# A hybrid attention and recurrence layer on one core: recurrence levels in pairs on two sets of key and query buffers, with moved loads, sigmoids and bias rows

## The chip, the core and the metric

The kernel runs on one core of one Trainium2 chip. A core has five engines with an instruction queue each: TensorE (PE, matmuls; PEld are its weight loads), VectorE (DVE), ScalarE (ACT), GpSimd (POOL) and SyncE (SP, which here only issues transfers), and 16 DMA engines move data between HBM and the on-chip memory (SBUF). Matmuls write to PSUM banks of 128 x 512 floats. The metric is the device time of one execution in microseconds (us); lower is better.

## The reference

One decoder layer on x of 1 x 1024 x 1024 in float32. The projection `h @ w_in` feeds two branches, which are gated and merged:

```python
mod = silu(c) @ w_ada + b_ada                      # shift, scale, gate
h = rmsnorm(x, norm_g) * (1 + scale) + shift
q_a, k_a, v_a, z_a, q_b, f_b, i_b, z_b, g_a, g_b = split(h @ w_in)
o_a = dilated_attention(q_a, k_a, v_a, rel_bias) * silu(z_a)       # 8 heads of 64
# recurrence, 8 heads, key and value width 128:
#   f = lb + (1 - lb) * sigmoid(f_b);  S_t = diag(f_t) S_(t-1) + (1 - f_t) i_t^T;  o_t = S_t^T silu(q_b)_t
o_b = rmsnorm(o_b, hgrn_onorm_g) * silu(z_b)
y = sigmoid(g_a) * (o_a @ w_branch_a) + sigmoid(g_b) * (o_b @ w_branch_b)
out = rmsnorm(x + gate * (y @ w_out), final_g)
```

The attention mixes three dilated windows; in the kernel this is one causal attention with a bias table (`toep`) that holds the relative bias and the logarithm of how many windows contain a distance.

## The kernel before

**Products.** All large products are done in two float parts, high and low: a step of a product is three 128x512 matmuls (`mm3`, lines 241, 242, 243: high by high, low by high, high by low). A weight piece of 128x512 is loaded (SP, L260), its high part is cast on ACT (`w_hi`, L248) and its low part subtracted on DVE (`w_lo`, L226). Products are done in pairs by a scheme with seven block products, whose sums run on DVE (L276) and copies on ACT (L329). They form a stream of steps. The attention and the recurrence are written as generators that yield an amount in microseconds; `fill(amount)` puts as many product steps of the stream between two pieces as `fill.rate` times the amount gives.

**Order.** PE's order is the order in which the program is written, throughout. In the start (lines 534 to 855) the orders of ACT, DVE and POOL are written by hand as well. Elsewhere a scheduler sets the orders of ACT, DVE, POOL and SP.

**Start (0 to some 76 us).** x arrives in eight tiles; each is squared and summed (`square_x`, L595/L597), the root taken with a power on POOL (`root_x`, L601), scaled (`scale_x`, L605 on ACT, L607 on DVE) and transposed (`turn_x` L624, `turn_late` L635). `mod_rows(c)` (L576) multiplies silu(c) with a quarter of w_ada that `load_wa(c)` loads, and copies the row (L579); `mod_turn(c)` (L586) turns it into columns, from which `make_h` (L650, L651, L654) makes the first operand `b11` (first half of the sequence) and `b12` (second half). `first_products` (L663, L664, L666) are the first three products, with weights that `split_first(n)` (L611) splits. `warm(n)` (L642) multiplies a tile of ones n times, to no use but keeping PE busy. `bias_row(b)` (L695) makes a third of the bias table on PE, `bias_add(b)` (L699) adds the logarithms on DVE.

**Attention (some 100 to 455 us).** Per head and query block: scores (L914, L915), bias and row maximum on DVE (L917), exp on ACT (L920), transposes, value products (L947). `load_head(h)` issues on POOL's queue the first half of a head's queries, keys and bias (`load_half`, L891, L897) and values (`load_value`, L902); the second half is loaded within `begin`. For head 0, the second half is held back by tiny casts on POOL (L889, L890) that read the first values tile `vq`. The values come from a turn (`ev_v`, L453 on ACT, L455 on SP) that writes a tile `vs` in SBUF and stores it to DRAM (`vq_d`).

**Branch a (some 455 to 555 us).** The attention output is gated and split (L1017 on DVE, L1019 on ACT) into operands `oah`, `oal`. Then `branch_a(m)`: `pre` loads g_a (L1029) and takes its sigmoid on ACT (L1030), when the unit's weights are prepared; `ev` multiplies the product with it, when the product ends.

**Recurrence (some 555 to 950 us, 8 heads).** The product of decays between two times is built by doubling: at level hl (1, 2, 4, ... 64) a block of 2 x hl times has keys in its first half and queries in its second. A level multiplies keys with queries (`small`, L1107, 32 matmuls of 32x32, or the wide form L1127 from 32 on), keeps the entries of that level (`copy_predicated`, L1120, or ACT copies into `amat`), multiplies the keys `kk` of the first halves (L1135) and the queries `qq` of the second halves (L1137; `qb` holds both queries and `qq`) with the decay of the other half, in place, and makes the decays of the next level (L1143, `tot`, `totn`). Each level ends with `yield 2.6`. Afterwards the keys are transposed (`kt`, L1159), the states made (`st`, L1171, L1175, L1177), the outputs (`pou`, L1186, L1188), their norm (L1191 to L1195; L1194 is a power on POOL) and, behind `yield 3.3`, their transposes (L1200) and the gate (L1202). The rest of the time, 950 to 1133, is branch b and the output product.

## Time and profile before

| what | value |
|---|---|
| time, median of 3 runs | 1131.35 us (1129.7 to 1131.97) |
| profiled execution | 1134.7 us |
| its span, first to last instruction | 1132.9 us |
| mean granted clock of TensorE | 0.994 |
| busy: PE, DVE, ACT, POOL | 1105.6, 807.6, 519.5, 123.1 us |

In the page's rows an engine's name stands ahead of its busy time, share of the span and number of instructions; small matmuls appear twice in the trace. The rows of a timeline have the start, the duration, the engine, the line and operation, out<-in with the shape and the count, and in brackets the idle time before and what ended it. Matmuls overlap, so the distance of two starts is the price of one, and not the duration. The rows of a stretch have the length, busy time and number of instructions, then the clock that TensorE was granted (1.00 is full), the share of the 16 DMA engines in use, and GB/s.

### The profile page before, as it was taken

What the parts mean: (1) busy time and instruction counts of PE and PEld (TensorE: products, weight loads), DVE (VectorE), ACT (ScalarE), POOL (GpSimd) and SP (SyncE); (2) the same over time, 40 slices, a digit from 0 to 9 for tenths busy, and PEclk for the clock granted to TensorE, in tenths of its full rate; (3) what the DMA queues carried; (4) which work ended last, traced back from release to release, by engine and by line L of the source; (5) the groups of instructions that cost most, each with busy time, mean ns of one, the idle gap of its engine ahead of it and who ended that gap; (6) DMA issues with size and microseconds to landing.
All of it is one profiled execution on the core that took longest, in us unless ns stands there. A gap on an engine that the chain in (4) does not pass through costs nothing.

```text
span 1132.9 us, 21754 instructions
## 1 busy us (share of the span) xinstructions
PE 1105.6 (98%) x8322; PEld 908.8 (80%) x8322; DVE 807.6 (71%) x1607; ACT 519.5 (46%) x1080; POOL 123.1 (11%) x207
## 2 busy tenths in 40 slices
PE   7999999999999999999999999999999999999997
PEld 6687788888888888788887878787887877888886
DVE  4487788878777776743788797978888773769053
ACT  5475555687555555632344444444453433334021
POOL 1103202303203201100000000000000012000000
PEclk9999999999999999999999999999999999999999
DMA  9739577646646624756725254443535389864052
GB/s 314 230 120 223 182 186 187 172 122 166 164 110 158 157 78 153 250 161 195 242 86 177 85 179 133 148 149 115 176 92 182 110 265 337 279 203 140 7 186 74
DMA packets 161608, 189.54 MB, mean 167 GB/s; under 512 B 11440, under 2 KB 107824, under 8 KB 161504
## 3 DMA queue, kind: packets, MB, share of 16 engines
q1 hardware_dynamic: 140080, 153.95, 42.5%
q0 software_dynamic: 21024, 33.60, 11.8%
q8 instruction: 65, 1.06, 0.4%
q10 hardware_dynamic: 400, 0.61, 0.2%
q14 instruction: 39, 0.32, 0.1%
HBM read 129.36 MB, written 58.76 MB: 166 GB/s over the span
## 4 chain that ended last, share of the span: by engine, by line
PE 88%; DVE 4%; DMA 3%; ACT 2%; issue 1%; POOL 1%; POOLq 0%; DVEq 0%; ACTq 0%; SPq 0%
PE m L241 18%; PE m L243 16%; PE m L242 16%; PE pq L243 5%; PE pq L242 5%; PE pq L241 5%; PE po L947 3%; PE pt L932 3%; PE pp L1107 3%; PE pss L915 1%; PE pss L914 1%; PE pou L1186 1%; DMA w_raw<-in_w_in_dram 1%; PE pou L1188 1%; PE pm L663 1%
## 5 line engine op out<-in xcount | busy, mean ns | idle before, releaser
L226 DVE TENSOR_TENSOR w_lo<-w_raw,w_hi 128x512 fp32r<-128x512 f32 x156 | 106.8, 687 | 55.5 <-ACT w_hi L248 52.5
L248 ACT CAST w_hi<-w_raw 128x512 fp32r<-128x512 f32 x146 | 90.5, 620 | 56.6 <-PE m L243 44.1
L329 ACT COPY ct<-m 128x512 f32<-128x512 f32 x90 | 52.7, 585 | 90.2 <-PE m L243 70.5
L248 ACT CAST w_hi<-w_s 128x512 fp32r<-128x512 f32 x90 | 55.9, 621 | 69.3 <-PE m L243 45.2
L276 DVE TENSOR_TENSOR ct<-m,ct 128x512 f32<-128x512 f32 x90 | 61.8, 687 | 24.6 <-PE m L243 24.2
L226 DVE TENSOR_TENSOR w_lo<-w_s,w_hi 128x512 fp32r<-128x512 f32 x90 | 61.9, 687 | 16.3 <-ACT w_hi L248 15.9
L920 ACT ACTIVATE s<-s,st 128x128 f32<-128x128 f32 (+3 forms) x64 | 49.8, 778 | 33.3 <-DVE st L917 33.3
L936 ACT CAST pth<-pt 128x512 fp32r<-128x512 f32 (+1 forms) x80 | 43.5, 544 | 36.6 <-PE pt L932 32.3
L226 DVE TENSOR_TENSOR ptl<-pt,pth 128x512 fp32r<-128x512 f32 (+1 forms) x80 | 50.6, 632 | 7.6 <-ACT pth L936 6.9
L1194 POOL TENSOR_TENSOR ssh<-ssh,halfh 128x4 f32<-128x4 f32 x16 | 18.0, 1128 | 340.4 <-DVE ssh L1193 340.4
L241 PE MATMUL m<-b11h,w_hi 128*128 128x512 f32 x124 | 52.4, 422 | 2.0 <-DVE ct L276 2.0
L241 PE MATMUL m<-b21h,w_hi 128*128 128x512 f32 x124 | 51.2, 413 | 0.0
L241 PE MATMUL m<-t2h,w_hi 128*128 128x512 f32 x120 | 49.9, 415 | 1.1 <-ACT ct L329 1.1
L241 PE MATMUL m<-b22h,w_hi 128*128 128x512 f32 x124 | 50.8, 410 | 0.0
L241 PE MATMUL m<-t1h,w_hi 128*128 128x512 f32 x120 | 50.2, 418 | 0.0
L241 PE MATMUL m<-t4h,w_hi 128*128 128x512 f32 x120 | 49.6, 413 | 0.4 <-DVE ct L276 0.4
L241 PE MATMUL m<-t3h,w_hi 128*128 128x512 f32 x120 | 49.6, 413 | 0.0
L243 PE MATMUL m<-b11l,w_hi 128*128 128x512 f32 x124 | 49.2, 397 | 0.0
L242 PE MATMUL m<-b11h,w_lo 128*128 128x512 f32 x124 | 49.2, 397 | 0.0
L243 PE MATMUL m<-b21l,w_hi 128*128 128x512 f32 x124 | 48.7, 393 | 0.0
L243 PE MATMUL m<-b22l,w_hi 128*128 128x512 f32 x124 | 48.7, 392 | 0.0
L242 PE MATMUL m<-b21h,w_lo 128*128 128x512 f32 x124 | 48.6, 392 | 0.0
(358 smaller groups left out, 3194.3 us busy)
## 6 DMA issues: line engine op xcount, KB each, us to landing
w_raw<-in_w_in_dram SPq DMA_DIRECT2D x128, 256.0 KB, 3.2
wa<-in_w_ada_dram SPq DMA_DIRECT2D x16, 512.0 KB, 8.9
qk_d<-ct SPq DMA_DIRECT2D x32, 256.0 KB, 4.2
k<-qk_d POOLq DMA_DIRECT2D x64, 128.0 KB, 4.7
toep<-toep_d POOLq DMA_DIRECT2D x16, 256.0 KB, 5.5
qp<-qk_d POOLq DMA_DIRECT2D x32, 128.0 KB, 4.9
vq_d<-ct SPq DMA_DIRECT2D x16, 256.0 KB, 3.5
vq<-vq_d POOLq DMA_DIRECT2D x16, 256.0 KB, 4.0
```

The costliest lines, as they stand in the source:

```text
L226: nc.vector.tensor_tensor(out_, a, hi.bitcast(F32), ALU.subtract)
L241: nc.tensor.matmul(ps, ah, bh, start=start, stop=False, skip_group_check=more)
L242: nc.tensor.matmul(ps, al, bh, start=False, stop=False, skip_group_check=more)
L243: nc.tensor.matmul(ps, ah, bl, start=False, stop=stop, skip_group_check=more)
L248: nc.scalar.copy(hi, src)
L276: nc.vector.tensor_tensor(out_, a, b_, op)
L329: nc.scalar.copy(c[name], b[which])
L920: nc.scalar.activation(s[:, :kw], s[:, :kw], AF.Exp, bias=prev, scale=-1.0, accum_out=st2[:, 2:3])
L932: nc.tensor.transpose(pt[:, c0:c0 + P], pn[b][:, kt * P:(kt + 1) * P], ident)
L936: nc.scalar.copy(pth[:, :w], pt[:, :w])
L947: nc.tensor.matmul(po[:, 256 - n:256], vq[kt // 4][:, kt % 4], src[:, c0:c0 + n], start=kt == 0 and a == 0, stop=kt == 2 * j + 1 and a == 1)
L1107: nc.tensor.matmul(pl[32 * b:32 * b + 32, c], kk[:, o:o + 32], qb[:, 2 - n:2, o:o + 32], start=True, stop=True)
```

## The change

- **Recurrence.** Level 1 runs alone, then levels (2, 4), (8, 16) and (32, 64) as pairs. A second pair of buffers for keys and queries (tiles named `kt` and `st`, whose memory later holds the transposed keys and the states; `st` has 8 slots now) takes what a level makes from the first: `grow` writes the multiplied halves into the other pair (DVE) and copies the unmultiplied halves (ACT). So within a pair both levels' operands exist at once and their matmuls are issued back to back. The second `grow` of a pair works in place. A head has eight new ACT copies of 128x512. The yield is 2.5 for each level, so 5.0 for a pair; the output's yield is 3.8, and the rate of filling is 34.0/34.6 of what it was.
- **First head's loads.** The second half's loads of head 0 are issued within `load_head(0)`, ahead of its value loads, and their casts read `vs`, the turn's tile in SBUF, in place of `vq`.
- **Sigmoid of branch a** is written in `ev`, ahead of the multiplication, in place of `pre`.
- **Start.** w_ada's first quarter is loaded ahead of the first weight piece; one bias row stays ahead of `mod_rows(0)`, one goes behind `mod_turn(0)`, one takes the place of ten of twelve warming matmuls. The first weight's cast and subtraction are taken apart and moved behind; the square of x7 and its root come ahead of the scalings; `mod_rows(1)` and `load_wa(3)` go ahead of the first products of the second half.
- **The turn of i** comes four product steps after its product in place of three.

The diff, cut: the old loop over the levels, which the section on the kernel before shows, and the bodies of `wide` and `keep`, which hold its matmuls from level 32 on and its copies unchanged, are left out, with two hunks of the start (the place of `load_wa(0)` and the bank of a bias row).

```diff
@@ -437,7 +437,7 @@
     def ev_k(p):
-    turned = {}
+    turned, last_v = {}, {}
     def ev_v(p, wait=2):
         def ev(src, th, psum):
@@ -453,6 +453,7 @@
                     nc.scalar.copy(vs[:, :, :, 0:E], got)
                     sub(vs[:, :, :, E:P], got, vs[:, :, :, 0:E])
                     nc.sync.dma_start(vq_d[p][:, 4 * th + n:4 * th + n + 2], vs.bitcast(F32))
+                    last_v[p] = vs
                 turned["v", p] = turned.get(("v", p), 0) + 1
             stream.after(wait, turn)
         return ev
@@ -469,7 +470,7 @@
-            stream.after(3, turn)
+            stream.after(4, turn)
@@ -606,12 +607,17 @@
+        def high_first(n):
+            firsts[n] = [wpool.tile([P, 4, P], F32R, name=name) for name in ("w_hi", "w_lo")]
+            nc.scalar.copy(firsts[n][0], stream.tiles[ids[n]])
+        def low_first(n):
+            sub(firsts[n][1], stream.tiles[ids[n]], firsts[n][0])
+            stream.done(ids[n])
-            hi, lo = (wpool.tile([P, 4, P], F32R, name=name) for name in ("w_hi", "w_lo"))
-            nc.scalar.copy(hi, stream.tiles[ids[n]])
-            sub(lo, stream.tiles[ids[n]], hi)
-            stream.done(ids[n])
-            firsts[n] = hi, lo
+            high_first(n)
+            low_first(n)
@@ -743,23 +748,22 @@
         scale_x(2, True)
         root_x(3)
         warm(8)
-        split_first(0)
         scale_x(3, False)
         turn_x(2)
         turn_x(3)
         keep_x(2)
         keep_x(3)
-        for b in range(2):
-            bias_row(b)
-        for b in range(2):
-            bias_add(b)
-        bias_row(2)
-        bias_add(2)
+        bias_row(0)
         mod_rows(0)
+        bias_add(0)
+        high_first(0)
         load_wa(2)
+        mod_turn(0)
+        bias_row(1)
+        low_first(0)
+        make_h(0, 0)
         stream.issue()
-        mod_turn(0)
-        make_h(0, 0)
+        bias_add(1)
         split_first(1)
         split_first(2)
         make_h(1, 0)
@@ -773,22 +777,24 @@
         root_x(4)
         root_x(6)
         root_x(5)
+        square_x(7, True)
+        root_x(7)
         scale_x(4, False)
-        square_x(7, True)
         scale_x(6, False)
-        root_x(7)
         scale_x(5, False)
         scale_x(7, True)
-        warm(12)
+        warm(2)
+        bias_row(2)
+        bias_add(2)
         turn_late(0)
-        main_banks(1)
-        first_products(0, (1,))
-        turn_late(1)
         mod_rows(1)
         load_wa(3)
-        first_products(1, (1,), (0,))
+        main_banks(1)
+        first_products(0, (1,), (0,))
+        turn_late(1)
+        first_products(0, (1,), (1, 2))
         mod_turn(1)
-        first_products(1, (1,), (1, 2))
+        first_products(1, (1,))
         make_h(2, 0)
         turn_late(2)
         first_products(2, (0,))
@@ -878,13 +884,16 @@
+            if h == 0:
+                load_half(h, 1)
         def load_half(h, c):
             if h == 0 and c == 1:
-                got = heads[h][4][0][:, 0, 0:1].bitcast(F32)
+                got = last_v[0][:, 0, 0, 0:1].bitcast(F32)
@@ -964,7 +973,8 @@
                     if i == 1:
-                        load_half(h, 1)
+                        if h > 0:
+                            load_half(h, 1)
@@ -1027,9 +1037,9 @@
-                    nc.scalar.activation(g[th], g[th], AF.Sigmoid)
             def ev(ps, th, psum):
+                nc.scalar.activation(g[th], g[th], AF.Sigmoid)
@@ -1099,55 +1109,77 @@
             dg = g1.tile([P, 256], F32, name="dg")
             d3 = c3(dg)
-            def small(n):
+            def small(n, k_, q_):
                 pl = pp.tile([P, 512], F32, name="pp")[:, :256 * n].rearrange("p (c n t) -> p c n t", c=8, n=n)
                 for c in range(8):
                     for b in range(4):
                         o = c * P + b * 32
-                        nc.tensor.matmul(pl[32 * b:32 * b + 32, c], kk[:, o:o + 32], qb[:, 2 - n:2, o:o + 32],
-                                         start=True, stop=True)
+                        to = pl[32 * b:32 * b + 32, c]
+                        if n == 2:
+                            nc.tensor.matmul(to, k_[:, o:o + 32], q_[:, :, o:o + 32], start=True, stop=True)
+                        else:
+                            nc.tensor.matmul(to[:, 0], k_[:, o:o + 32], q_[:, o:o + 32], start=True, stop=True)
                 return pl
...
+            def wide(hl, k_, q_):
...
+            def keep(hl, pl):
...
+            def halves(t, hl):
+                return t.rearrange("p (n two t) -> p n two t", two=2, t=hl)
+            def grow(fq, hl, a, b_):
+                n = S // (2 * hl)
                 t3 = fq[:, :2 * n].rearrange("p (n two) -> p n two", two=2)
+                for i in range(2):
+                    nc.vector.tensor_tensor(halves(b_[i], hl)[:, :, i], halves(a[i], hl)[:, :, i],
+                                            t3[:, :, 1 - i:2 - i].to_broadcast([P, n, hl]), ALU.mult)
+                    if a is not b_:
+                        nc.scalar.copy(halves(b_[i], hl)[:, :, 1 - i], halves(a[i], hl)[:, :, 1 - i])
+                tn = tots[hl.bit_length() % 2]
+                nc.vector.tensor_tensor(tn[:, :n], t3[:, :, 0], t3[:, :, 1], ALU.mult)
+                return tn
+            tots = tot, g1.tile([P, S // 2], F32, name="totn")
+            here, there = (kk, qq), (g1.tile([P, S], F32, name="kt"), g1.tile([P, S], F32, name="st"))
+            for levels in ((1,), (2, 4), (8, 16), (32, 64)):
+                got = []
+                if len(levels) == 2:
+                    fq = grow(fq, levels[0], here, there)
+                for hl, (k_, q_) in zip(levels, (here, there)):
+                    got.append(small(2, k_, qb) if hl == 1 else (small(1, k_, q_) if hl <= 16 else wide(hl, k_, q_)))
+                for hl, pl in zip(levels, got):
+                    keep(hl, pl)
+                if len(levels) == 2:
+                    fq = grow(fq, levels[1], there, there)
                 else:
+                    fq = grow(fq, 1, here, there)
+                here, there = there, here
+                yield 2.5 * len(levels)
+                if 4 in levels:
                     load_z(h)
+                if 16 in levels and h + 1 < NHB:
                     load_f(h + 1)
             for b in range(4):
                 nc.vector.tensor_copy(am[32 * b:32 * b + 32, :, 32 * b:32 * b + 32], d3[32 * b:32 * b + 32])
@@ -1161,7 +1193,7 @@
-            st_ = g1.tile([P, 7, P], F32, name="st")
+            st_ = g1.tile([P, 8, P], F32, name="st")
@@ -1193,7 +1225,7 @@
-            yield 3.3
+            yield 3.8
@@ -1210,7 +1242,7 @@
-        fill.rate = (len(stream.steps) - stream.at - 4) * 4 / NHB / 34.0
+        fill.rate = (len(stream.steps) - stream.at - 4) * 4 / NHB / 34.6
```

How the instructions stand on each engine, at three places. First PE in the start, from the last transposes of the first four x tiles (L624, now L630) to the first products (L663, now L669); L695 is a bias row and now L701, L576 is `mod_rows` and now L577, L586 is `mod_turn` and now L587. Before:

```order
L624 MATMUL pm_0_279<-kc,x_147 128x128 x4
L695 MATMUL pxt<-oh,rb 8x384
L695 MATMUL pmod<-oh,rb 8x384
L695 MATMUL pxt<-oh,rb 8x384
L576 MATMUL pmod<-wa_159,scz 32x256 x4
L576 MATMUL pmod<-wa_161,scz 32x256 x4
L576 MATMUL pmod<-wa_163,scz 32x256 x4
L576 MATMUL pmod<-wa_165,scz 32x256 x4
L586 MATMUL pmod<-kc,row 128x2 x2
L663 MATMUL pm_0_352<-b11h,w_hi 128x512
L664 MATMUL pm_0_352<-b11h,w_lo 128x512
L666 MATMUL pm_0_352<-b11l,w_hi 128x512
```

With the change:

```order
L630 MATMUL pm_0_275<-kc,x_147 128x128 x4
L701 MATMUL pxt<-oh,rb 8x384
L577 MATMUL pmod<-wa_157,scz 32x256 x4
L577 MATMUL pmod<-wa_159,scz 32x256 x4
L577 MATMUL pmod<-wa_161,scz 32x256 x4
L577 MATMUL pmod<-wa_163,scz 32x256 x4
L587 MATMUL pmod<-kc,row 128x2 x2
L701 MATMUL pxt<-oh,rb 8x384
L669 MATMUL pm_0_348<-b11h,w_hi 128x512
L670 MATMUL pm_0_348<-b11h,w_lo 128x512
L672 MATMUL pm_0_348<-b11l,w_hi 128x512
```

Two of the three bias rows have left the place ahead of `mod_rows(0)`; one of them stands behind `mod_turn(0)`. Further on, the second half of the start begins like this with the change (L648 is a warming matmul, L641 a late transpose):

```order
L672 MATMUL pm_0_350<-b11l,w_hi 128x512
L648 MATMUL pxt<-ones 128x128 x2
L701 MATMUL pxt<-oh,rb 8x384
L641 MATMUL pxt<-kc,t4h 128x128 x2
L641 MATMUL pxt<-kc,t4l 128x128 x2
L577 MATMUL pmod<-wa_177,scz 32x256 x4
L577 MATMUL pmod<-wa_179,scz 32x256 x4
L577 MATMUL pmod<-wa_181,scz 32x256 x4
L577 MATMUL pmod<-wa_183,scz 32x256 x4
```

Where twelve warming matmuls stood there are two and a bias row, and `mod_rows(1)` comes before any product of the second half.

Second, the recurrence. On PE, two levels of one head before, `pp` being the bank of a level's result, `kk` and `qb` its keys and queries:

```order
L1107 MATMUL pp<-qb,kk 32x32 x32
L241 MATMUL m_7214<-b21h,w_hi 128x512
L242 MATMUL m_7214<-b21h,w_lo 128x512
L243 MATMUL m_7214<-b21l,w_hi 128x512
L241 MATMUL m_7001<-t3h,w_hi 128x512
L242 MATMUL m_7001<-t3h,w_lo 128x512
L243 MATMUL m_7001<-t3l,w_hi 128x512
L241 MATMUL m_7001<-t3h,w_hi 128x512
L242 MATMUL m_7001<-t3h,w_lo 128x512
L243 MATMUL m_7001<-t3l,w_hi 128x512
L1107 MATMUL pp<-qb,kk 32x32 x32
L241 MATMUL m_7001<-t3h,w_hi 128x512
```

And a pair with the change (L1122; `kt` and `st` are the second pair of buffers):

```order
L243 MATMUL m_7261<-b21l,w_hi 128x512
L241 MATMUL m_7261<-b21h,w_hi 128x512
L242 MATMUL m_7261<-b21h,w_lo 128x512
L243 MATMUL m_7261<-b21l,w_hi 128x512
L1122 MATMUL pp<-qb,kk 32x32 x32
L1122 MATMUL pp<-st,kt 32x32 x32
L241 MATMUL m_7261<-b21h,w_hi 128x512
L242 MATMUL m_7261<-b21h,w_lo 128x512
L243 MATMUL m_7261<-b21l,w_hi 128x512
```

Nine product matmuls stood between two levels; now the two stand side by side. On DVE, between one pair's matmuls and the next pair's, in the same head (L1155 is the multiplication in `grow`, L1160 the next decays, L1139 the predicated copy; L226 and L276 belong to products):

```order
L276 TENSOR_TENSOR w_s<-w_s,w_raw_6213 128x512
L1139 COPY_PREDICATED dg<-kc,pp 128x256 x2
L1155 TENSOR_TENSOR kt<-kt,tot 128x32x16
L1155 TENSOR_TENSOR st<-st,tot 128x32x16
L226 TENSOR_TENSOR w_lo<-w_s,w_hi 128x512
L1155 TENSOR_TENSOR kk<-kt,totn 128x16x32
L276 TENSOR_TENSOR w_s<-w_raw_6147,w_s 128x512
L1155 TENSOR_TENSOR qb<-st,totn 128x16x32
L1160 TENSOR_TENSOR tot<-totn 128x16
```

Two predicated copies and four multiplications now follow each other, with product operations among them; before, one predicated copy and two multiplications stood between two levels.

Third, ACT in branch a, the casts of `oah` and the first sigmoids. Before (L1019 the cast, L1030 the sigmoid):

```order
L1019 CAST oah_4914<-oar 128x512
L329 COPY ct<-m_5032 128x512
L248 CAST w_hi<-w_raw_4948 128x512
L1030 ACTIVATE oar<-oar 128x512
L1019 CAST oah_4912<-oar 128x512
L1030 ACTIVATE oar<-oar 128x512
L1019 CAST oah_4914<-oar 128x512
L248 CAST w_hi<-w_s 128x512
L1030 ACTIVATE oar<-oar 128x512
```

With the change (L1029 the cast, L1042 the sigmoid):

```order
L1029 CAST oah_4904<-oar 128x512
L329 COPY ct<-m_5022 128x512
L248 CAST w_hi<-w_raw_4938 128x512
L1042 ACTIVATE oar<-oar 128x512
L1029 CAST oah_4902<-oar 128x512
L1042 ACTIVATE oar<-oar 128x512
L1029 CAST oah_4904<-oar 128x512
L248 CAST w_hi<-w_s 128x512
L1042 ACTIVATE oar<-oar 128x512
```

The scheduler's order is the same in both, though the sigmoid is written at another place.

60 lines of the change are left out of this document (20 added, 40 removed).

## The prediction

> **What bounds the kernel now.** I read the page first, then the waits of TensorE (PE), then stretches of the span with the granted clock beside the busy time. From the page, its engine row and its chain row:
>
> ```profile
> PE 1105.6 (98%) x8322; PEld 908.8 (80%) x8322; DVE 807.6 (71%) x1607; ACT 519.5 (46%) x1080; POOL 123.1 (11%) x207
> PE 88%; DVE 4%; DMA 3%; ACT 2%; issue 1%; POOL 1%; POOLq 0%; DVEq 0%; ACTq 0%; SPq 0%
> ```
>
> PE is the bound: 1105.6 of 1132.9 us, and 88% of the chain. So this edit can gain in three ways only: less idle time of PE (27.3 us, and it includes the first loads), fewer or closer matmuls, fewer stretches at a low clock. The waits, PE's line and tile, the releaser, then total us, times, longest:
>
> ```profile
> PE pss L914 <- DVE st L917: 2.5, 1, 2.5
> PE m L241 <- DVE ct L276: 2.5, 2, 2.0
> PE pt L1200 <- DVE kt L1195: 2.1, 2, 1.4
> PE pm L663 <- ACT b11h L650: 1.4, 1, 1.4
> PE m L241 <- ACT ct L329: 1.1, 1, 1.1
> PE pm L663 <- ACT b12h L650: 0.9, 1, 0.9
> PE pp L1127 <- DVE qb L1137: 0.6, 1, 0.6
> PE pm L663 <- ACT b11h L654: 0.5, 1, 0.5
> PE pp L1107 <- DVE qb L1137: 0.5, 1, 0.5
> ```
>
> One long wait each at the first attention score (L914) and in branch a (L241 for DVE's L276), three in the start (L663), and little in the recurrence (L1107, L1127, L1200). Waits cost more than their length. In these windows stand PE's time, its busy time and instructions, clock, DMA share, GB/s:
>
> ```profile
> 23.80:27.22 3.42, 1.75 (x6) 1.00 1.07 360
> 27.22:30.63 3.41, 3.41 (x10) 0.50 1.10 349
> 119.38:122.79 3.41, 0.91 (x4) 1.00 0.25 89
> 122.79:126.20 3.41, 3.27 (x13) 0.50 0.47 153
> 470.95:474.37 3.42, 1.37 (x7) 1.00 0.42 160
> 474.37:477.78 3.41, 3.41 (x8) 0.50 0.63 224
> ```
>
> Three times a window of 3.41 us in which PE is busy half or less is followed by 3.41 us at half clock. The last row holds 8 matmuls, 0.43 us each; the rows of the next fence start them 0.22 to 0.23 apart. Such a window therefore costs 8 x 0.20 = 1.6 us on top of the wait.
>
> **Part 1, the recurrence.** Rows of one level and of the product matmuls around it (start, duration), then the group's row:
>
> ```profile
> 616.33 0.39 PE L242 MATMUL m<-t3h,w_lo 128*128 128x512 f32 x1
> 616.55 0.39 PE L243 MATMUL m<-t3l,w_hi 128*128 128x512 f32 x1
> 616.87 0.76 PE L1107 MATMUL pp<-qb,kk 128*32 128x32 f32 x64
> 617.57 0.50 PE L241 MATMUL m<-b11h,w_hi 128*128 128x512 f32 x1
> 617.90 0.40 PE L242 MATMUL m<-b11h,w_lo 128*128 128x512 f32 x1
> L1107 PE MATMUL pp<-qb,kk 128*32 128x32 f32 x2048 | 24.4, 199 | 0.6 <-DVE qb L1137 0.5
> ```
>
> Going from 512-column matmuls to the small set and back costs time beyond the set. Entry: 616.55 to 616.87 is 0.32 instead of 0.23, +0.09. Leaving: the 64 records span 0.76 us and one takes 0.199, so they start (0.76 - 0.199)/63 = 0.009 apart; the next product could have followed 0.58 after 616.87, and came after 0.70, +0.13 (0.12 and the rounding). The first product after the set: 617.57 to 617.90 is 0.33 instead of 0.23, +0.10. Together 0.32 us for a switch. The change runs levels 2 and 4, 8 and 16, 32 and 64 back to back: 4 switches a head in place of 7, 24 fewer over 8 heads: **-7.7 us**. Bounds: -5 if the back-to-back sets have a seam of a third of a switch, -7.7 if none.
>
> What it adds on the other engines: eight copies of 128x512 on ACT for each head, 8 x 8 x 0.585 (the L329 row of the page, a copy of that size) = 37 us of ACT. Busy us of PE, PEld, DVE, ACT, POOL through six heads, and through the stretch in which DVE is fullest:
>
> ```profile
> 620.00:900.00 280.00, 277.42 (x3278) 225.65 (x3277) 229.98 (x446) 119.25 (x294) 13.50 (x12) 1.00 0.42 134
> 606.00:620.00 14.00, 13.48 (x240) 10.53 (x239) 13.51 (x26) 5.38 (x9) 0.00 (x0) 1.00 0.74 240
> L1120 DVE COPY_PREDICATED dg<-kc,pp 128x256 f32<-128x256 int32 x27 | 12.0, 443 | 2.1 <-PE pp L1107 2.0
> L1135 DVE TENSOR_TENSOR kk<-kk,tot 128x512 f32<-128x512 f32 x22 | 15.0, 683 | 0.1
> ```
>
> ACT goes from 119 of 280 to 119 + 6 x 8 x 0.585 = 147: it has room, so the copies are costed at nothing. If ACT were late, the second set of a pair would wait for a half that no product covers. DVE has less room, 82%, and its work per pair becomes one chain: 2 predicated copies and 4 multiplies, 2 x 0.44 + 4 x 0.60 (multiplies on DVE overlap: 0.68 long, 0.60 apart) = 3.3 us. In DVE's program order up to four product operations (0.6 each) stand inside that chain, so 3.3 to 5.7. The cover is 21 product matmuls at 0.228 = 4.8, and 0.6 of the sets themselves, 5.4. So a pair waits 0 to 0.3 on this account, 24 pairs: 0 to +7. Most pairs have at most two such operations inside (up to 4.5): I take **+1.5**.
>
> The last head's output transposes wait now:
>
> ```profile
> 945.50 0.63 PE L1200 MATMUL pt<-kc,kt 128*128 128x128 f32 x4 [1.36 <-DVE kt L1195]
> ```
>
> Nine product matmuls stand between its output products and these transposes; with the yield at 3.8 and a lower rate there are 15: 6 x 0.228 = 1.37, **-1.4** (0 if what follows DVE is late by as much). The other waits of L1107, L1127 and L1200 are 0.5 + 0.6 + 0.7 = 1.8; intervals of 5.0 in place of 2.6 cover about half: **-1** (0 to -1.8). Recurrence: -7.7 + 1.5 - 1.4 - 1 = **-8.6** (all better ends -10.9; all worse ends -5 + 7 = +2).
>
> **Part 2, the start.** Rows of PE, and one of ACT:
>
> ```profile
> 18.25 0.81 PE L695 MATMUL pxt<-oh,rb 32*8 32x384 f32 x2
> 20.44 1.94 PE L576 MATMUL pmod<-wa,scz 128*32 128x256 f32 x32
> 24.89 0.50 PE L663 MATMUL pm<-b11h,w_hi 128*128 128x512 f32 x1 [1.42 <-ACT b11h L650]
> 36.13 0.50 PE L663 MATMUL pm<-b12h,w_hi 128*128 128x512 f32 x1 [0.87 <-ACT b12h L650]
> 33.27 1.15 ACT L605 ACTIVATE t4l<-t4l,rs 128x1024 f32<-128x1024 f32 x1 [3.27 <-POOL rs L601]
> ```
>
> Three bias rows, from 18.25 up to mod_rows(0) at 20.44, (20.44 - 18.25)/3 = 0.73 each, stand on PE ahead of the modulation that the first product waits for; one is left: -1.5. The split of the first weight gives up its place on DVE ahead of the scaling of x3: -0.7 (one 128x512 subtraction, as long as the L1135 row's). So the first product comes at some 22.7 instead of 24.89, and the chain behind it moves with it: squares on ACT, powers on POOL, the last scaling on ACT (33.27 to 34.42) and the late transposes behind that. Ten of twelve warming matmuls go and a bias row comes in their place: nothing by itself, since the transposes wait for that scaling either way. mod_rows(1) then runs (1.9 us, as the first does) while ACT makes b12h, for which PE waited 0.87: -0.9. The wait for b11h of L654, 0.5, is covered likewise: -0.5. A bias addition that is now ahead of the second weight's split on DVE: +0.5. That makes -1.5 - 0.7 - 0.9 - 0.5 + 0.5 = -3.1. And the first half-clock window (27.22) may go, since its cause, the window with 1.75 us busy, holds that wait of 1.4 and may shrink with the work ahead of it: -1.6 as a whole, at an even chance -0.8. I take **-4** (-6 to -1: up to two of the small terms may fail, and the two warming matmuls leave PE without work for 1 to 2 us near 30, where another half-clock window would cost +1.6).
>
> The Trainium skill, page "TensorE: Matmul & The Clock Gate", section "HAM oscillation — how this bites in real kernels", puts the loss of clock behind idle gaps over about 3.4 us; by it, the thinner warm-up costs nothing. The windows above do not agree: no wait in the list is over 2.5 us, and three half-clock windows follow. By the page the start is -3.1 without regard to the clock, by the rows it is -4.7 or -1.5, as one window goes or one comes.
>
> **Part 3, the first head's loads.** DMA share in two stretches, three pieces of the chain of waits, and the first of the loads on POOL:
>
> ```profile
> 92.00:100.00 8.00, 6.87 (x35) 1.00 0.76 228
> 100.00:112.00 12.00, 12.00 (x58) 1.00 1.09 252
> 102.56 11.89 DMA w_raw<-in_w_in_dram
> 100.85 0.18 POOL L889 CAST qp<-vq 128x1 fp32r<-128x1 f32 x1 [0.83 <-DMA vq<-vq_d]
> 92.72 0.37 ACT L453 CAST ct<-pt 128x256 fp32r<-128x256 f32 x1 [0.55 <-DVE ct L226]
> ```
>
> From 100 on the DMA engines are full; a weight load issued at 102.56 takes 11.9 us, the chain that starts there ends at the score's 2.5 us wait, and a half-clock window follows: 2.5 + 1.6 = 4.1 to be had. The seven moved loads (one of 256 KB, six of 128 KB, 1 MB; at 252 GB/s some 4 us of traffic) go out behind L889's casts, which wait for vq until 100.85. Their gate becomes the v turn's tile in SBUF, which ACT writes at 92.72 to 93.09: they go some 7 us earlier, where the share is 0.76. On POOL's queue they pass the value load, which starts later by their issue. The weight then lands perhaps 4 us sooner, more than the wait. I take **-3** of -4.1 (to +1, if they lengthen the other wait here, the 1.1 for ACT's L329 near 96).
>
> The page "DMA: Bandwidth & Descriptors", section "Issuing engines are not separate DMA queues", of the Trainium skill says that all issuers share 16 engines and interleave. By that rule the megabyte merely takes its time elsewhere.
>
> **Part 4, the sigmoid at use.** Now ACT waits for a load ahead of casts that the products need:
>
> ```profile
> 471.73 0.63 ACT L1030 ACTIVATE oar<-oar 128x512 f32<-128x512 f32 x1 [5.79 <-DMA oar<-ga_d]
> 474.34 0.75 PE L241 MATMUL m<-b11h,w_hi 128*128 128x512 f32 x1 [2.05 <-DVE ct L276]
> ```
>
> 2.05 + 1.6 = 3.7 us would go. But ACT's order is set by the scheduler, and it puts each sigmoid at the very place among the casts where it was. **-0.7**, the gain only if the load lands earlier by chance (bounds -3.7 and 0). The i turn one product later moves four transposes by 0.7 us beside products: 0.
>
> **Sum.** -8.6 - 4 - 3 - 0.7 = -16.3. The profiled execution took 1134.7 (span 1132.9), so 1118.4 (span 1116.6); the median of the runs, 1131.35, lies 3.35 below it, and becomes **1115**.
>
> **The rivals.** (a) *The pair's second set waits* (slower). If ACT's copies or DVE's chain end late at each of the 24 pairs, 16.3/24 = 0.68 us of wait undoes everything; at the 0.9 by which a chain of 5.7 passes 4.8 of cover alone, it is -16.3 - 1.5 + 21.6 = +3.8: 1135. For it: DVE is busy 13.51 of 14 us in one stretch. Against it: 82% over six heads, and few operations inside most chains. (b) *Start and loads give nothing*: a half-clock window takes the place of the start's waits, and the loads fill the DMA engines 7 us earlier instead of later. Then only -8.6 - 0.7 are left: 1122; with the loads alone in vain, 1118. For it: the DMA share is 0.76 already where they go. (c) *Branch a's wait goes too*, by an earlier landing, and the start keeps its clock: -16.3 - 3 - 2 = -21.3: 1110. Against it: ACT's order. (d) *The switches do not get cheaper*, the seam between two sets being as dear: -16.3 + 7.7: 1123; with (b), 1130. For it: no row shows two different sets back to back. Against it: in the rows a switch costs beside a 512-column matmul. That part 4 does not do what it says is in the forecast.
>
> **How the numbers follow.** Forecast 0.52; (c) 0.18; (b) or (d) 0.19; both, no change, 0.04; (a) 0.07. The time is the forecast's, 1115. The range goes down past (c) with the recurrence's better end, 1106, and up past (b) and (d), 1125. A measurement here tells about 0.2% (2.3 us) from no change: faster 0.89, same 0.04, slower 0.07.
>
> **What would show it.** Right: 32 sets of small matmuls instead of 56, product matmuls before and after them as above and no wait of L1122 or L1131 over 0.5; mod_rows(1) ahead of the first late product; the first score's wait under 1 us and full clock after it; the 2-us wait of branch a still there. Wrong: PE waits for kt, st, kk or qb at most pairs; half-clock windows at new places near 30; ACT's or DVE's share in the recurrence at 95%.

## The result and the profile after

The changed kernel takes 1123.45 us (median of 4 runs, 1121.71 to 1124.08) against 1131.3 (4 runs, 1129.7 to 1131.97): a ratio of 0.9937, 95% interval 0.9924 to 0.995. In a second comparison it took 1121.94 (6 runs) against 1129.84 (29 runs), ratio 0.9932, 0.9917 to 0.9947. So it is faster by 0.6 to 0.7%: 7.1 to 7.7 us by the ratios, 7.9 by the medians, where 16.3 us were forecast. The direction and the range (1106 to 1125) held; the size is less than half. Two executions far outside the rest, 1461 us of the kernel before and 3850 us of an experiment below, are left out of all comparisons.

The profiled execution took 1122.96 us, with a span of 1121.1: 11.8 less than the span before. The engine row of its page, and seven of the waits of PE (line and tile, releaser, that is what ended the wait, then total us, times, longest):

```profile
PE 1095.0 (98%) x8302; PEld 905.4 (81%) x8302; DVE 806.8 (72%) x1607; ACT 555.2 (50%) x1144; POOL 124.6 (11%) x207
```

```profile
PE m L241 <- issue: 1.9, 1, 1.9
PE m L241 <- DVE ct L276: 1.9, 4, 0.9
PE pt L1232 <- ACT ct L470: 1.8, 1, 1.8
PE m L242 <- issue: 1.5, 1, 1.5
PE m L241 <- ACT w_hi L248: 1.2, 1, 1.2
PE pp L1122 <- DVE qb L1155: 1.0, 1, 1.0
PE pp L1122 <- issue: 0.4, 1, 0.4
```

The wait of 2.5 us for the first scores is gone, and a new one, for a weight's cast (L248), stands some 20 us ahead of its place. The 2.0 us wait of branch a is gone too. New is a releaser that the list of before does not have for PE: "issue", time in which PE waited for nothing that the profile shows, 1.9 + 1.5 + 0.4 us.

To see where time went, I cut each trace at the starts of the same PE instructions: the first product of the stream (L241), the last value product of the attention, the first small matmul of the recurrence, the first product of branch b (`pq`). Stretches in us, of the two profiles of before (the second belongs to an experiment below) and two of the change, counted from PE's first instruction, 1.0 us after the span's start:

```
                    start   products+attention   branch a   recurrence   end
before              76.26   364.75               116.45     390.40       176.62
before, again       78.89   364.53               113.55     390.27       177.08
change              71.89   362.60               113.87     386.43       177.90
change, again       71.42   363.21               114.52     386.35       176.99
```

The start lost 4.4 us against the profile on which the forecast was made, the attention 2.1, branch a 2.6, the recurrence 4.0, and the end gained 1.3. Forecast were 4, 3, 0.7, 8.6 and 0.

### The profile page after: what moved, and what is told of

It reads as the page before. It is cut to its first block, busy times and chain, and to the rows that moved or that the text cites. A ratio compares the mean times of both kernels' runs of the same rounds, so it can differ in the third digit from the quotient of the medians.

```text
span 1121.1 us, 21828 instructions
## 1 busy us (share of the span) xinstructions
PE 1095.0 (98%) x8302; PEld 905.4 (81%) x8302; DVE 806.8 (72%) x1607; ACT 555.2 (50%) x1144; POOL 124.6 (11%) x207
## 4 chain that ended last, share of the span: by engine, by line
PE 78%; DVE 8%; issue 7%; DMA 3%; ACT 2%; POOL 1%; POOLq 0%; DVEq 0%; ACTq 0%
PE m L241 15%; PE m L243 15%; PE m L242 15%; PE pq L241 4%; PE pq L242 4%; PE pq L243 4%; PE po L956 2%; PE pt L941 2%; PE pp L1122 2%; PE pss L924 1%; PE pss L923 1%; DVE w_lo L226 1%; PE pou L1218 1%; PE pm L669 1%; PE pm L672 1%
## 5 line engine op out<-in xcount | busy, mean ns | idle before, releaser
L226 DVE TENSOR_TENSOR w_lo<-w_raw,w_hi 128x512 fp32r<-128x512 f32 x156 | 106.7, 686 | 61.2 <-ACT w_hi L248 60.7
L248 ACT CAST w_hi<-w_raw 128x512 fp32r<-128x512 f32 x146 | 90.5, 621 | 43.0 <-PE m L243 29.7
L248 ACT CAST w_hi<-w_s 128x512 fp32r<-128x512 f32 x90 | 55.9, 621 | 56.4 <-PE m L243 37.5
L329 ACT COPY ct<-m 128x512 f32<-128x512 f32 x90 | 52.6, 585 | 57.3 <-PE m L243 52.8
L276 DVE TENSOR_TENSOR ct<-m,ct 128x512 f32<-128x512 f32 x90 | 61.7, 686 | 24.4 <-PE m L243 24.1
L226 DVE TENSOR_TENSOR w_lo<-w_s,w_hi 128x512 fp32r<-128x512 f32 x90 | 61.7, 686 | 12.3 <-ACT w_hi L248 11.4
L226 DVE TENSOR_TENSOR ptl<-pt,pth 128x512 fp32r<-128x512 f32 (+1 forms) x80 | 50.5, 631 | 7.4 <-ACT pth L945 6.6
L241 PE MATMUL m<-t4h,w_hi 128*128 128x512 f32 x120 | 49.5, 412 | 3.3 <-issue 1.9
L241 PE MATMUL m<-b11h,w_hi 128*128 128x512 f32 x124 | 50.8, 410 | 0.2 <-DVE ct L276 0.2
L241 PE MATMUL m<-b22h,w_hi 128*128 128x512 f32 x124 | 50.9, 410 | 0.0
L241 PE MATMUL m<-t3h,w_hi 128*128 128x512 f32 x120 | 49.5, 412 | 1.2 <-ACT w_hi L248 1.2
L241 PE MATMUL m<-b21h,w_hi 128*128 128x512 f32 x124 | 50.5, 408 | 0.0
L242 PE MATMUL m<-b22h,w_lo 128*128 128x512 f32 x124 | 48.5, 391 | 1.5 <-issue 1.5
L241 PE MATMUL m<-t2h,w_hi 128*128 128x512 f32 x120 | 49.2, 410 | 0.6 <-ACT ct L329 0.6
L241 PE MATMUL m<-t1h,w_hi 128*128 128x512 f32 x120 | 49.4, 412 | 0.3 <-DVE ct L276 0.3
```

The costliest lines, as they stand in the source:

```text
L226: nc.vector.tensor_tensor(out_, a, hi.bitcast(F32), ALU.subtract)
L241: nc.tensor.matmul(ps, ah, bh, start=start, stop=False, skip_group_check=more)
L242: nc.tensor.matmul(ps, al, bh, start=False, stop=False, skip_group_check=more)
L248: nc.scalar.copy(hi, src)
L276: nc.vector.tensor_tensor(out_, a, b_, op)
L329: nc.scalar.copy(c[name], b[which])
```

## The experiments

**The two kernels once more.** First the kernel before, unchanged.

> The kernel before, unchanged, profiled once more. Theory A (the profiled execution of before was longer than its other runs because branch a's load came late in it): the wait of L241 for DVE's L276 in branch a is under 1 us here, the first score's wait of 2.5 us is there again, and the span is about 1129.5. Rival B (both waits belong to the kernel): the wait of 2 us and the half-clock window behind it are there again, and the span is about 1133.

Span and clock of its profiled execution, and two of PE's waits in it:

```profile
core 0: 1132.7 us, clock 0.991
```

```profile
PE pss L914 <- DVE st L917: 2.5, 1, 2.5
PE m L241 <- DVE ct L276: 0.8, 2, 0.4
```

Theory A's first half holds: the first scores wait again, branch a does not. Its second half, a span of 1129.5, does not hold: the start took 2.6 us more, with 13.7 us at half clock (19.3 to 33.0) where the first profile had 3.4. The timed runs say why one profile is a poor base here. The 37 runs of the kernel before in this comparison (29 of the reference, 8 of this copy), by the granted clock that each lists:

```
clock            runs   median us   range
0.991 to 0.994     6    1134.3      1132.9 to 1137.2
0.995              8    1131.1      1129.1 to 1132.9
0.996              8    1129.65     1127.6 to 1133.9
0.997, 0.998      15    1129.15     1127.3 to 1131.4
```

The profile that the forecast used had 0.994: it belongs to the slowest sixth.

The Trainium skill, page "TensorE: Matmul & The Clock Gate", section "Part 1: The HAM clock gate", says that the window in which activity is watched is free-running and does not begin with the kernel. The traces agree: in the first profile the half-clock stretches begin 3.3 us past a multiple of 3.413 us from the first instruction (27.2, 122.8, 474.4), in the second 2.2 us past one (19.3, 125.1). Which idle time is followed by such a stretch is not settled by that. The kernel with the recurrence's part alone (below) has two windows of this kind, each with a wait of 1.9 us and nearly the same busy time, and full clock behind the first (it has 1.00 from 120.65 on), half clock behind the second:

```profile
117.24:120.65 3.41, 1.58 (x7) 1.00 0.56 202
642.90:646.31 3.41, 1.54 (x10) 1.00 0.51 187
646.31:649.72 3.41, 3.41 (x11) 0.50 0.68 246
```

Then the change, unchanged.

> The change, unchanged, once more. Theory A (PE runs out of instructions: its three stalls with no releaser all stand at instruction 256 k + 448, where a fetched block of 256 begins): stalls without a releaser, 2 to 5 us in all, in the recurrence again and at instructions of that form, though their length may differ, since the fetch shares the DMA engines; time 1123.5. Rival B (a disturbance of that one execution): no such stall, or at other counts, and a span about 4 us shorter, 1117.

It took 1121.94 us, with 3.3 us of waits without a releaser: theory A.

**What PE waits for when it waits for nothing.** In the change, two pairs of level sets and what follows them (start, duration, idle time before with its releaser):

```profile
751.51 0.76 PE L1122 MATMUL pp<-qb,kk 128*32 128x32 f32 x64
752.12 0.75 PE L1122 MATMUL pp<-st,kt 128*32 128x32 f32 x64
754.78 0.39 PE L241 MATMUL m<-t4h,w_hi 128*128 128x512 f32 x1 [1.90 <-issue]
...
842.55 0.76 PE L1122 MATMUL pp<-st,kt 128*32 128x32 f32 x64
843.21 0.75 PE L1122 MATMUL pp<-qb,kk 128*32 128x32 f32 x64
843.90 0.50 PE L241 MATMUL m<-b22h,w_hi 128*128 128x512 f32 x1
845.90 0.39 PE L242 MATMUL m<-b22h,w_lo 128*128 128x512 f32 x1 [1.50 <-issue]
```

Both stand behind a pair. Of the DMA queues just ahead of the first of these gaps and in its beginning, 751.6 to 753.5 us (packets, MB, share of 16 engines):

```profile
q8 instruction: 1, 0.02, 5.2%
```

That one packet is PE's instructions: 65 packets of 16,384 bytes on this queue in the whole execution, for 16,783 recorded instructions of PE and its weight loads, 256 to a packet. Counting those instructions from the start and numbering the packets k = 0, 1, ..., I find each packet's start, its end, and where the longest gap between two PE instructions near it falls:

```
profile            k    packet us         PE's gap stands at count    gap us
change             27   599.55-600.54     256 x 27 + 448              0.6
change             42   751.77-753.36     256 x 42 + 448              2.0
change             50   843.57-844.55     256 x 50 + 448              1.9
change, again      27   601.01-601.98     256 x 27 + 448              1.1
change, again      37   704.30-705.25     256 x 37 + 448              0.7
change, again      42   754.04-755.17     256 x 42 + 448              1.4
change, again      50   843.40-845.12     256 x 50 + 448              1.0
```

Each gap stands at the very instruction 256 k + 448, and ends 1.1 to 1.4 us after packet k has landed. In quiet stretches a packet starts when PE is some 155 instructions past 256 k, so PE has 293 more before it runs dry. A pair takes 256 of them within 1.3 us (128 records of matmuls and as many of weight loads). No record shows when a packet is asked for. If it is at that instruction 155, and PE can go on 1.4 us after the landing, then from asking to use takes 3.3 to 6.9 us in this stretch (an estimate from the packets' times; tenth to ninetieth percentile of 32 packets). Level 1's 128 instructions and the first pair's 256 are only 9 to 12 product matmuls apart. Of the Trainium skill, the page "Runtime: NRT & Kernel Launch", section "Instruction fetch mechanics", says that instructions come in blocks of 16 KiB, 256 of them, which the packets confirm; it also says that this fetch is hidden, since issue is slower than the filling, and the rows above show the opposite for dense small matmuls.

**Shifting the count.** If this is right, only the count of instructions ahead matters.

```diff
         warm(20)
+        ps = px.tile([P, 512], F32, name="pxt")
+        for n in range(58):
+            b = n % 4 * 32
+            nc.tensor.matmul(ps[b:b + 32, 0:32], ones[:, 0:32], ones[:, 0:32], start=True, stop=True)
```

> The change with 58 tiny matmuls (32x32, of ones) at a place in the first 12 us where PE waits for x: they cost no time, but every later instruction of PE comes 232 places later, so that the boundaries of fetched blocks fall on others. Theory A (PE stalls where a block of 256 instructions begins while the fetch is late, at 256 k + 448 by count): the stalls at 601, 752 and 844 us are gone, any new ones stand at 256 k + 448 of the new count; worked out from the trace, boundaries with less than 5.5 us between trigger and need are 3 in place of 7, so 1 to 3 us less than the change: 1119 to 1121. Rival B (a pair of sets stalls by itself, whatever the count): the same three places, 1122.

The gaps at 42 and 50 are gone, and the only ones left without a releaser, 0.8 us in two, stand at other places (the larger at 256 x 33 + 448, the smaller at 256 x 37 + 448). From the waits in the recurrence, 560 to 935 us:

```profile
PE pt L1236 <- ACT ct L470: 1.8, 1, 1.8
PE pp L1126 <- DVE qb L1159: 1.0, 1, 1.0
PE pp L1126 <- issue: 0.8, 2, 0.6
```

The recurrence took 383.55 us in place of 386.4, 2.9 less. The time is 1120.51 (ratio 0.9903, 0.9882 to 0.9925), 1.4 less than the change in the comparison before: my tiny matmuls were not free. They stood ahead of transposes whose x was already there, and the first product of the stream came at 74.50 in place of 71.4 to 71.9. So I put them behind `warm(4)`, where PE waits 1.4 us for x1 in every profile above.

> The change with the 58 tiny matmuls behind the four warming ones, where PE waits 1.4 us for x1 in every run, in place of behind the first twenty, where they delayed the start by 2.1 us. Theory A (the count alone takes the stalls for instructions away, worth 2.9 us in the recurrence): start as in the change, 71 to 72.5, recurrence 383 to 384, time 1118.5 to 1120. Rival B (what the recurrence gains comes back elsewhere): 1121 or more.

1120.01 us (0.991, 0.989 to 0.993); recurrence 382.73, start 72.39, no wait without a releaser of over 0.3 us. The recurrence's 3.7 us are confirmed; of the time 1.9 us arrive. In the profile the rest went to a wait of 1.9 us of the first `pq` products for DVE (`gbr`) with a half-clock stretch of 3.41 us behind it; whether the ordinary run has that too is not shown.

**Spreading the levels.**

```diff
-                yield 2.5 * len(levels)
+                yield 4.0 if 64 in levels else 4.5
```

> The change with yields of 4.5, 4.5, 4.5 and 4.0 behind the four groups of levels, in place of 2.5, 5, 5 and 5: more product matmuls between level 1 and the first pair, fewer between pairs. Theory A (256 + 128 instructions of level 1 and the first pair within 4 us are what drains PE's store of instructions): stalls without a releaser under 1 us in all, 1 to 3 us less than the change, 1119 to 1121. Rival C (the chain on DVE fills the interval between pairs): waits of the small matmuls for kt, st, kk or qb rise to 3 us or more, 1123 or more.

No wait without a releaser is left, and the first waits of the recurrence are

```profile
PE pt L1232 <- ACT ct L470: 1.8, 1, 1.8
PE pt L1232 <- DVE kt L1227: 0.9, 2, 0.8
PE pp L1131 <- DVE tot L1160: 0.6, 1, 0.6
```

The recurrence took 382.42 us. Waits of small matmuls for DVE are 0.8 us in all: rival C, DVE's chain, is out. The time is 1120.47 (0.9905, 0.9884 to 0.9927), with 2 to 3 us given back behind the recurrence (end 179.92).

**The recurrence alone, and all but the recurrence.** The first is the kernel before with the hunks of the diff from `dg = g1.tile` on; the second is the change without them.

> The kernel before with the recurrence's part of the change alone. Theory A (the switches saved 7.6 us as forecast, 1.6 come back at seams between the two sets of a pair and 3 to 5 as stalls for instructions): 3 to 5 us less than before, 1126 to 1128, with stalls without a releaser behind pairs. Rival B (the forecast's sum for the recurrence holds, and the rest of the change gave less than its profile shows): 8.6 less, 1122.7. Rival C (DVE's chain outlasts the cover): waits of L1122 for kt, st, kk or qb of 5 us or more in all.

> The change with the recurrence as before: start, first loads, sigmoid and the turn of i alone. Theory A (start -4.4 and attention -2.1 as the two profiles show, branch a the same in an ordinary execution): 5 to 7 less than before, 1124.5 to 1126.5. Rival B (forecast's recurrence): only about 0 to 2 less, 1129.5 to 1131, so that the whole is 1123.5 with -8.6 in the recurrence.

The recurrence alone gives 1128.29 (ratio 0.9985, 0.9972 to 0.9998), the rest alone 1127.82 (0.9981, 0.997 to 0.9992). Neither theory had this: -1.7 and -2.1 by the ratios do not add up to -7.7. The traces explain a part. The rest alone leaves out 40 PE instructions in the start (ten warming matmuls), and in it the old recurrence stalls for instructions too, within a set:

```profile
755.84 0.73 PE L1117 MATMUL pp<-qb,kk 128*32 128x32 f32 x60
757.62 0.26 PE L1117 MATMUL pp<-qb,kk 128*32 128x32 f32 x4 [1.05 <-issue]
```

This is at 256 x 41 + 448; its recurrence took 391.35 us, 1.0 more than before. The recurrence alone took 388.19, with a half-clock stretch at 646 us behind a wait of 1.9 us for ACT's L469 (the change has that wait, 1.8 us, without the stretch), and with 2.0 us of stalls in four places, the longest, 1.0, at 256 x 27 + 448. I tried to take the stall out of the rest alone.

> The change with the recurrence as before and ten tiny matmuls in the first 12 us, which give every later instruction of PE the place that it has in the kernel before, modulo 256. Theory A (the change's 40 instructions less in the start had brought a stall for instructions into the old recurrence too, and so the parts alone gave less than the whole): the stall near 755 is gone, 0.5 to 1.5 us less than without them: 1126.3 to 1127.3. Rival B: the same time, 1127.8, and the stall at the same place.

The stall is gone and the recurrence took 390.09 us, as before, but the time is 1127.96: ten of these 12 runs had a clock of 0.995 or less, where the rest alone without the tiny matmuls had 0.997 in the middle. They stand where they cost time in the first shift above, and the profiled start took 72.50 in place of 70.74. So the shift of the count is confirmed in its stretch and not in the time. By the profiles the stall and the half-clock stretch would make up between 2 and 3 of the 3.9 us between the parts' sum and the whole; in the times none of it was recovered, and the 3.9 us stay unexplained there.

**The first head's loads.** The change with `load_half(h, 1)` and its gate back at their old places:

```diff
             load_half(h, 0)
-            if h == 0:
-                load_half(h, 1)
             load_value(h, 0)
...
-                got = last_v[0][:, 0, 0, 0:1].bitcast(F32)
+                got = heads[h][4][0][:, 0, 0:1].bitcast(F32)
...
-                        if h > 0:
-                            load_half(h, 1)
+                        load_half(h, 1)
```

> The change with the first head's second half of loads where it was before. Theory A (the moved loads only moved the contention: the wait for the first scores went, and one for a weight's cast near 102 came): 0 to 1 us more than the change, 1122 to 1123, with the 2.5 us wait for DVE's L926 back and the one for ACT's L248 gone. Rival B (the forecast: 3 us): 1124.5 to 1125.5.

It took 1119.89 us (0.9899, 0.9877 to 0.9921): less than the change, not more, by 2.1 us against the second comparison's median (1121.94) and by some 4 by the ratios, which come from different comparisons; the stretches below bear out the 2. Both expectations were wrong in sign. The stretch of products and attention is 360.93 us in place of 362.6 and 363.2. The profiles of the other experiments agree: with the new start it took 360.9 to 361.7 us in all five without the moved loads, and 362.4 to 364.1 in all seven with them. The change has

```profile
102.03 0.51 PE L241 MATMUL m<-t3h,w_hi 128*128 128x512 f32 x1 [1.18 <-ACT w_hi L248]
```

and without the moved loads that wait is gone, while the one for the first scores, 2.5 us in before, is

```profile
114.67 0.50 PE L921 MATMUL pss<-k,qp 128*128 128x512 f32 x1 [0.28 <-DVE st L924]
```

So the start's part of the change had already dissolved most of it; nothing else of the change acts before 115 us (the first turn of i comes at 426). The wait for the cast, of 0.8 to 2.2 us, is in all eight profiles with the moved loads and in none of the nine without. Where the 1.2 us come from: ACT's rows ahead of that cast, and, of the transfers issued from 86 to 106 us, stores of turned values and loads of weights (how many, size, median us from issue to landing), in the change

```profile
95.06 0.65 ACT L453 CAST ct<-pt 128x256 fp32r<-128x256 f32 x2 [1.35 <-DMA vq_d<-ct]
...
100.88 0.59 ACT L329 COPY ct<-m 128x512 f32<-128x512 f32 x1 [3.73 <-PE m L243]
101.36 0.62 ACT L248 CAST w_hi<-w_raw 128x512 fp32r<-128x512 f32 x1
```

```profile
vq_d<-ct SPq DMA_DIRECT2D x8, 256.0 KB, 5.8
w_raw<-in_w_in_dram SPq DMA_DIRECT2D x5, 256.0 KB, 4.5
```

and without the moved loads

```profile
93.78 0.65 ACT L453 CAST ct<-pt 128x256 fp32r<-128x256 f32 x2 [1.05 <-DVE ct L226]
...
97.87 0.59 ACT L329 COPY ct<-m 128x512 f32<-128x512 f32 x1 [1.93 <-PE m L243]
98.35 0.62 ACT L248 CAST w_hi<-w_raw 128x512 fp32r<-128x512 f32 x1
```

```profile
vq_d<-ct SPq DMA_DIRECT2D x8, 256.0 KB, 4.0
w_raw<-in_w_in_dram SPq DMA_DIRECT2D x6, 256.0 KB, 8.3
```

The weights do land sooner with the move. What lands later are the stores of the turned values, which run beside it: one issued at 89.31 has its last piece down at 94.96, 5.65 us later, where without the move the same store takes 3.76 (88.68 to 92.44); the next takes 6.58 (94.20 to 100.78) against 4.00 (93.77 to 97.77). Each holds a `ct` buffer, and ACT's next write of a `ct` begins 0.1 us after that last piece: 95.06 and 100.88 in the change, 97.87 without the move. For the copy the view names PE, which had ended its product at 98.11 in the change, so the buffer is the better reading. Behind the copy in ACT's queue stands the weight's cast, and PE waits for the cast. This chain is read from the two traces; giving the stores more buffers was not tried.

The rule that I set against the forecast (the Trainium skill, "DMA: Bandwidth & Descriptors", "Issuing engines are not separate DMA queues") agrees with these rows in kind: loads issued by POOL lengthened stores issued by SP, by 1.9 and 2.6 us.

**The start.** The change with the start as before, and 54 tiny matmuls that keep the count of instructions modulo 256:

> The change with the start as before, and 54 tiny matmuls that keep the place of all later instructions modulo 256. Theory A (the start gave what the two profiles show, 4.4 to 5): 1126 to 1127.5, start of the first L241 product near 76. Rival B (the profiled start of before was disturbed by half-clock windows, and an ordinary one is only 2 to 3 us longer): 1124 to 1125.5.

1128.26 us (ratio 0.9992, 0.9977 to 1.0007; 12 runs from 1126.11 to 1132.9), some 6 more than the change: theory A in sign, and a little above its upper end. Its tiny matmuls delayed the start little, if at all: the transposes of x0 begin at 8.31 us, in the four other profiles with the old start at 7.81 to 8.41. In its profile the first product came not near 76 but at 81.02, with 17.1 us at half clock (17.8 to 34.8). And though the start is the old one, the wait for the first scores is gone here too: the moved loads do take it away, as the forecast said, where the start has not done so. The stalls for instructions stand at packets 28, 43 and 51, one later than in the change, as 256 more instructions ahead of them ask for. With the start's old order four of its runs had a clock of 0.989 to 0.993; none of the change's ten had less than 0.995.

**Filling the wait before the scores.** In the kernel before, ahead of the scores that wait 2.5 us:

```diff
                     fill(apart)
+                    if n == 1:
+                        for q in range(58):
+                            g = q % 4 * 32
+                            nc.tensor.matmul(po2[g:g + 32, 1, 0:32], ident[:, 0:32], ident[:, 0:32], start=True, stop=True)
+                        for q in range(6):
+                            nc.tensor.matmul(po2[:, 1, 0:P], ident, ident, start=True, stop=True)
```

> The kernel before with 64 matmuls to no use (58 of 32x32, 6 of 128x128, 256 instructions, so that the count modulo 256 is kept) where PE waits 2.5 us for the first scores' bank. Theory A (a window of 3.41 us that is half idle brings the half-clock window behind it): no half-clock window at 122 to 129 us in the profile, 0 to 1.6 us less than before, 1128.3 to 1129.8, as far as the phase of the windows brings it in an ordinary execution. Rival B (the half clock there has another cause): the window is there again, time unchanged at 1129.8 or, if the useless matmuls delay the scores, longer.

Length, busy time, clock, DMA share and GB/s of two stretches; first the second profile of before, then this kernel:

```profile
122.00:126.00 4.00, 1.49 (x5) 0.89 0.28 93
126.00:130.00 4.00, 4.00 (x18) 0.69 0.43 154
```

```profile
122.00:126.00 4.00, 3.59 (x119) 1.00 0.69 239
126.00:130.00 4.00, 4.00 (x57) 1.00 0.54 180
```

In this execution the half clock is gone where PE is kept busy, as theory A has it; but one execution cannot show the cause, since a wait of 1.9 us at the same place brought no half clock either (the first row of the recurrence's part alone, above). The time did not fall: 1131.49 (median of 11 runs; ratio 1.0003, 0.9986 to 1.002). So in ordinary runs the wait and its window, as far as they have it, are worth too little to be seen.

**Versions without the two faults.** Without the moved loads, and with the tiny matmuls behind `warm(20)`, with the spread yields, with the tiny matmuls behind `warm(4)`, and with yields of 4.5 and the turn of i after six product steps:

> The change without the moved loads and with the 58 tiny matmuls that shift the count of instructions. Theory A (the two causes, the loads' contention and the stalls for instructions, are separate): the 2 to 2.5 us of the one and the 1.4 to 2 us of the other add up, 1117.5 to 1118.5, with at most 1 us of stalls without a releaser. Rival B (they share a cause, a full set of DMA engines): no better than either alone, 1119.9.

> The change without the moved loads and with the yields 4.5, 4.5, 4.5 and 4.0. Theory A: no stall without a releaser of over 0.5 us, the recurrence as short as with these yields before (382.4 us from its first small matmul), but some 2 to 3 us of waits for DVE behind it, since its order has changed there: 1117 to 1119. Rival C: waits for DVE take the place of the stalls, 1120 or more.

> The change without the moved loads and with the 58 tiny matmuls behind the four warming ones. Theory A (loads and stalls are separate causes, and only the place of the tiny matmuls kept them from adding up in time): 1116.5 to 1118. Rival B: 1119.9, as without the shift.

> The change without the moved loads, with a yield of 4.5 behind each group of levels, and with the turn of i after six product steps in place of four, so that in no head an i turn stands three matmuls ahead of output transposes that need the same bank. Theory A (that order costs the 1.8 us wait of L1232 for ACT's L470): that wait is gone, no stall without a releaser over 0.5 us: 1116.5 to 1118.5. Rival B (other waits come in its place): 1119.3 or more.

In this order: 1120.0 (0.9911, 0.9894 to 0.9928), 1119.26 (0.9899, 0.9883 to 0.9916), 1118.52 (0.9893, 0.9875 to 0.9911) and 1118.67 (0.9891, 0.9871 to 0.991). The first shows nothing, since its tiny matmuls cost the start what the recurrence won (recurrence 382.58, start 74.39). The third is 1.4 us better than without the shift, less than the 2 to 3 us of theory A; in its profile the end has a 1.8 us wait for DVE. In the fourth the wait that it was to remove came back in another head, 2.45 us long:

```profile
590.64 0.66 PE L1229 MATMUL pt<-kc,kt 128*128 128x128 f32 x4 [2.45 <-ACT ct L470]
```

so the order on PE was not the cause. In the change, the rows of ACT around that wait (PE from 638.4 to 640.18):

```profile
638.53 0.62 ACT L1236 CAST ct<-zs 128x512 fp32r<-128x512 f32 x1 [2.45 <-DVE zs L1234]
639.06 0.58 ACT L329 COPY ct<-m 128x512 f32<-128x512 f32 x1
639.53 0.59 ACT L470 COPY ct<-pt 128x512 f32<-128x512 f32 x1
```

The copy that frees the bank stands in ACT's queue behind a cast that waits 2.45 us for DVE. This is read from one trace and was not tried by itself. All four are faster than the kernel before, and by 1.9 to 3.4 us faster than the median of the change, which was taken in another comparison; the last two, and the one with spread yields, can't be told apart.

## Why the prediction was wrong

Of the 16.3 us 7.9 came, 8.4 less. Between the profiles 4.6 are missing in the recurrence and 0.9 in the attention, the end lost 1.3, and the start and branch a gave 2.3 more than forecast. The other 3.9 are the base.

**The base.** The step "the median of the runs, 1131.35, lies 3.35 below it" was treated as a constant. It was not one: the profiled execution had three half-clock stretches and a late load in branch a, and the forecast took credit for removing them: 1.6 us of the window in part 3, 0.8 in the start, 0.7 in branch a. An ordinary run has fewer. At a clock of 0.997 the whole span has some 6.8 us at half clock (an estimate from the clocks), and the last 3.2 to 4.1 us of both profiles of before are at half clock anyway; that leaves room for one stretch, and at 0.996 for less than two. Which of the three an ordinary run has is not shown. This is why the spans differ by 11.8 us and the medians by 7.9.

**Part 1, -8.6; measured -4.0 between the profiles.** The main term was right: entering and leaving sets, and the first product behind them, cost 7.6 us less (summed over the gaps between those kinds of instructions in both traces; -7.7 forecast). What failed is that the sum had no term for two things that came back. The seams within pairs cost 1.7 us: 0.12 each at the change from level 32 to 64, and 0.05 at the others; the bound had allowed 2.7, the sum none. And 3.8 us went to waits for instructions, a cost that stood in no term and no rival. I had asked what each other engine and queue would do with the denser sets and not where PE's own instructions come from. Both ways of taking these waits away shortened the recurrence, by 2.9 and 3.7 (two places of the tiny matmuls) and 4.0 us (the spread yields). The other waits fell from 5.4 us to 4.2: 1.2 less, where the forecast had 0.9 less. Rival (a), DVE's chain, did not come: 1.0 us of L1122 for `qb`, and none for the pairs' other operands.

**Part 2, -4; measured -4.4 between profiles and some -6 in time.** The first product came at 21.90 (forecast 22.7), mod_rows(1) covers b12h without a gap:

```profile
32.71 1.93 PE L577 MATMUL pmod<-wa,scz 128*32 128x256 f32 x32
34.57 0.50 PE L669 MATMUL pm<-b12h,w_hi 128*128 128x512 f32 x1
```

The half-clock window was not removed in either profile of the change (22.7 and 23.7), but long stretches of it became rare: of the five profiles with the old start three have 13.7 to 17.1 us at half clock there, and none of the twelve with the new start has more than 6.8. That the time gained more than the sum fits this. The prediction's reading that a window with PE busy half or less is followed by half clock does not hold: in the change PE is busy for 1.65 of the 3.41 us from 637.09 on, around a wait of 1.8, and the clock behind it is full.

**Part 3, -3; measured +2.** The step "the weight then lands perhaps 4 us sooner" held (median 4.5 us in that stretch, 11.6 before) and was worth nothing, because the wait that it was to remove had gone for another reason, the new start: the sum counted the two parts as independent. What failed besides is that I looked at what the load is moved out of and not at what it is moved into: it lengthened stores of the values and held up a copy on ACT by 3.0 us (2.4 without the 0.65 by which this profile was already later at 86 us). The term's upper bound, "to +1, if they lengthen the other wait here, the 1.1 for ACT's L329", had the copy that was hit, and half its price. Rival (b) named this for the loads, at 1118 with the rest intact; it gave "nothing", not a loss.

**Part 4.** The sigmoid's move did nothing, as forecast, since ACT's order did not change: branch a took 113.87 and 114.52 us, against 113.55 where before had no late load. The 2 us wait was one execution's; the forecast that it would "still be there" was wrong for that reason.

**The signs to watch.** "No wait of L1122 or L1131 over 0.5" failed once, with a wait of 1.0; the 2 us wait of branch a was not there; 32 sets, the first scores' wait and the start came as said.

## What to carry to other kernels

Profile the kernel before twice, or look at the granted clock of its timed runs, before crediting a change with removing a stall: what one execution shows may belong to that execution. A dense run of tiny matmuls has a price that neither its own duration nor the waits of before show: count the instructions, 256 to a fetched block here, and spread them, as the yields of 4.5 did here, where PE would use up what it holds before the next block can land. A load that is moved out of a busy stretch lands in another, so look at what is stored and loaded there, which buffers those transfers hold, and who waits for them.

## What the runs showed of the hardware

PE ran dry of instructions at fixed places: 256 k + 448 by count, with a restart 1.1 to 1.6 us after the 16 KB block had landed. The packet itself took 0.9 to 2.5 us in the recurrence of the change, while other queues moved data; from asking to use is 3.3 to 6.9 us by the estimate above. A shift of 40 or 232 instructions at the start of the program therefore brought or removed stalls of up to 2 us some 600 to 800 us later, in an otherwise unchanged part. And a half-clock stretch of 3.41 us (some 1.6 us of time by the prediction's estimate) followed a wait of 1.9 us in one place of an execution (646 us) and not in another (121 us).
